# A diffusion layer's scan, projections and feed-forward: projections of the next group dealt over all steps, outputs turned a step later, low parts of weights on VectorE, and tanh of the feed-forward's first pair ahead of half the sums

## The chip, the cores and the metric

The kernel runs on one core of a Trainium2 chip. The metric is the device time of one execution in microseconds (us). The kernel before took 1807.36 us in the median of 3 runs (1804.32, 1807.36 and 1807.61). Engines are named as the profile names them: PE (TensorE matmul) and PEld (its weight loads), DVE (VectorE), ACT (ScalarE), POOL (GpSimd), SP (SyncE, which issues the DMAs).

## The reference, cut to what matters

One layer of a hybrid backbone for 640 tokens (128 of context, 512 latent), model width 1024, all in fp32:

```
h = rms_norm(x) * (1 + scale1) + shift1
q, k, v, conv_bg, conv_cg, conv_x, z, xbc, dt_raw, gate_logits = split(h @ w_in)
y_attn = blocked_attention(rope(rms_norm(q)), rope(rms_norm(k)), v) @ w_attn_o
y_conv = (conv_bg * conv3(conv_cg * conv_x)) @ w_conv_o
xs, bm, cm = split(silu(conv3(xbc) + b))          # 8 groups of 4 heads, state 128
dt = softplus(dt_raw + dt_bias)                   # the decays of the scan come from dt
y_f, s_f = ssd_chunked(xs, dt, ...)               # chunks of 128 tokens, forward
y_b, s_b = ssd_chunked(reversed, ...)             # and backward
y_ssd = rms_norm((y_f + y_b + d * xs) * silu(z)) @ w_ssd_o
x = x + gate1 * ((g_attn * y_attn + g_conv * y_conv + g_ssd * y_ssd) @ w_merge)
h = rms_norm(x) * (1 + scale2) + shift2
x = x + gate2 * ((silu(h @ w1_gate) * (h @ w1_up)) @ w2)
```

A chunk's part of the scan is a product of its C and B with the decay between each two tokens (y within the chunk), a state that the chunk adds, and C times the state that came in.

## The kernel before, in words

**Precision and tiles.** Every fp32 product is three matmuls, high by high, high by low and low by high part. `split` makes the parts: ACT casts the high part (L163), and the engine `low` subtracts it for the low part (L164), which is DVE unless the caller passes `low=pool`. Weights come in slabs of 4 × 128 × 256 through `wload` (raw tile `wr`, parts `wh` and `wl`). Tokens lie along the free axis, 640 in two halves of 320, so that a block of 256 outputs takes 2 × 8 × 3 × 2 = 96 matmuls of 128x320 (`fblock`, L297). `acc` is a pair of PSUM banks, `mx` one bank; `psum(n)` opens a pool with n of the first kind and 8 − 2n of the second.

**Order of the work.** The engines work in order, and the order on each is the one in which the program issues, save that `urgently` and `tc.high_priority()` pull an instruction forward. Where two pieces of work share PE, one is a generator (`yield` after each piece) and the other advances it with `next`. A tile of a pool with n buffers can be written when the reader of the n-th last one is done.

**The stages.** (1) 0 to 52 us: modulation and the normed h. (2) To 290 us: projections. Two plain gates, and between them `sum_forms` (L267), which makes the sums T1 to T4 of h's quarters: per block two subtractions on DVE (L274, L276) and two additions on POOL (L275, L277), and their parts. Then 12 conv units and 3 gate units go through `sunit`, a Strassen form with 7 products of 12 matmuls (L241) instead of 96; after most products DVE combines the banks into `uv` (L536 is the helper that records it, urgent). `decays()` is a generator that makes dt and what follows from it on DVE, advanced with `next(dec)` after each unit. (3) To 520 us: attention, with parts of the remaining gates, `spare`, as filling. (4) To 1047 us: the scan, in 8 groups. `group_scan(this)` (from L897) yields 9 times; its turns (`turn`, L890: x and B of a chunk, by PE), states (L912), carries of the state (`pv`, L917 and L919), weights (decay matrix `M`: a mask on POOL, L928, exponentials on ACT, L934, products on DVE), outputs (L948 and L954 on PE; y on DVE, L955 to L962) and `turn_back` (L970: y turned back by PE, two scaled copies on ACT). After each step the loop at the end advances `group_proj(g + 1)` once: a block of x0, x1, B, C or two z blocks of 24 matmuls of 128x256 (L283 to L285), seven pieces for nine steps. At step 5 `begin` turns two chunks of the next group. The last group has the spare gates beside it, three parts a step. (5) To 1268 us: the branches' output products and their merge, while `modulate()` computes the second modulation on DVE (L1074, rows `aw` from memory, two buffers). (6) To 1400 us: the merged projection, norm, and the feed-forward's first pair (gate and up of block 0) as plain halves (L1216) with `sum_forms` between, on POOL and DVE. Then `banks.close()` gives their four pairs of banks back and `psum(0)` makes eight single ones. (7) To the end: ten more pairs of blocks through `sunit` (`ff_gate`, `ff_up`) and the products down.

## Time and profile before

| | |
|---|---|
| median of 3 runs | 1807.36 us |
| profiled execution, its own time | 1801.9 us |
| its span | 1800.0 us (1.9 us lie beside it) |
| PE busy | 1731.0 us, 11924 instructions |
| DVE busy | 1280.1 us, 2256 instructions |
| ACT busy | 791.5 us |
| POOL busy | 424.5 us, 317 instructions |
| mean granted clock of PE | 0.989 |

A row of a wait reads: engine, tile and line that waited, behind the arrow what released it, then total us, times and longest. A row of a group reads: line, engine, operation, tile written and read, shape, number, then busy us and the mean ns of one, then the idle time of the engine before them and what ended it. A row of the timeline: start, length, engine, line, operation, tile, shape, number, and in brackets the idle time before it. A row `60/70/80` of a line gives the shortest, median and longest ns of one. The granted clock is a share of full speed.

### The profile page before, as it was taken

To read this page: it belongs to the slowest core of one execution; us is meant where nothing else is said; L and a number is where in the kernel's file an instruction comes from. 1 tells how busy PE (TensorE), PEld (TensorE's weight loads), DVE (VectorE), ACT (ScalarE), POOL (GpSimd) and SP (SyncE) were. 2 spreads that over 40 slices of the span, in tenths; PEclk is the share of its full clock that TensorE was granted. 3 is DMA by queue.
4 is the path that set the end of the run, shared out by engine and by line. 5 is a ranking of instruction groups with operands and counts; after the bars stand their busy time and mean duration, and the time that the engine had idled before them with its cause. 6 is when DMAs were issued, how large, how long until landed. Compare 5 with 4: busy or idle time off the path is not lost.

```text
span 1800.0 us, 30404 instructions
## 1 busy us (share of the span) xinstructions
PE 1731.0 (96%) x11924; PEld 1669.0 (93%) x11924; DVE 1280.1 (71%) x2256; ACT 791.5 (44%) x1592; POOL 424.5 (24%) x317
## 2 busy tenths in 40 slices
PE   7999999999999999999999999999997999999999
PEld 3899999999999898889889989999997999999999
DVE  5788786786546777777678557877778767767685
ACT  4534443465454665556565432122255423324240
POOL 0344451110134334333331000000004232322320
PEclk9999999999999999999999999999999999999999
DMA  7633333211243433433343378865551323223222
GB/s 286 206 101 114 111 99 115 86 42 54 77 124 111 115 100 109 140 105 102 109 130 115 110 262 269 267 194 159 172 166 48 94 59 94 71 82 95 71 89 76
DMA packets 112831, 221.76 MB, mean 123 GB/s; under 512 B 9584, under 2 KB 53488, under 8 KB 111664
## 3 DMA queue, kind: packets, MB, share of 16 engines
q1 hardware_dynamic: 112688, 219.82, 38.5%
q8 instruction: 94, 1.54, 0.3%
q14 instruction: 49, 0.40, 0.1%
HBM read 193.67 MB, written 26.12 MB: 122 GB/s over the span
## 4 chain that ended last, share of the span: by engine, by line
PE 71%; DVE 16%; DMA 7%; issue 3%; ACT 2%; POOL 1%; SPq 0%; DVEq 0%; ACTq 0%; POOLq 0%
PE mx L241 22%; PE acc L297 21%; PE mx L297 10%; DMA aw<-in_ada_dram 5%; PE mx L283 3%; PE mx L284 3%; PE mx L285 3%; DVE wl L164 2%; DVE jk L1074 2%; PE mx L912 2%; PE mx L954 1%; DVE y L961 1%; PE mx L403 1%; PE acc L725 1%; PE mx L948 1%
## 5 line engine op out<-in xcount | busy, mean ns | idle before, releaser
L297 PE MATMUL acc<-h,wh 128*128 128x320 f32 x1984 | 377.2, 312 | 0.7 <-ACT s L782 0.5
L163 ACT CAST wh<-wr 128x1024 fp32r<-128x1024 f32 (+2 forms) x226 | 218.1, 968 | 272.8 <-PE mx L241 83.8
L297 PEld LDWEIGHTS acc<-h,wh 128*128 128x128 f32 x1984 | 311.3, 189 | 1.4 <-ACT s L782 0.6
L164 DVE TENSOR_TENSOR wl<-wr,wh 128x1024 fp32r<-128x1024 f32 (+1 forms) x178 | 219.2, 1233 | 49.9 <-ACT wh L163 48.4
L297 PE MATMUL acc<-h,wl 128*128 128x320 f32 x992 | 230.1, 312 | 3.5 <-DVE wl L164 3.5
L241 PE MATMUL mx<-h,wh 128*128 128x320 f32 x840 | 188.9, 313 | 11.3 <-ACT s L163 11.3
L297 PEld LDWEIGHTS acc<-h,wl 128*128 128x128 f32 x992 | 167.1, 189 | 4.8 <-DVE wl L164 4.8
L164 POOL TENSOR_TENSOR wl<-wr,wh 128x1024 fp32r<-128x1024 f32 x48 | 119.2, 2489 | 189.4 <-ACT wh L163 183.9
L283 PE MATMUL mx<-wh,h 128*128 128x256 f32 x560 | 160.9, 287 | 1.7 <-ACT wh L163 1.0
L285 PE MATMUL mx<-wh,h 128*128 128x256 f32 x560 | 158.4, 283 | 0.0
L284 PE MATMUL mx<-wl,h 128*128 128x256 f32 x560 | 158.3, 283 | 0.0
L297 PE MATMUL acc<-s,wh 128*128 128x320 f32 x768 | 152.7, 310 | 4.3 <-issue 2.4
L241 PEld LDWEIGHTS mx<-h,wh 128*128 128x128 f32 x840 | 142.5, 190 | 11.8 <-ACT s L163 11.5
L241 PE MATMUL mx<-s,wh 128*128 128x320 f32 x640 | 141.6, 309 | 0.0
L163 ACT CAST wh<-ws 128x512 fp32r<-128x512 f32 (+1 forms) x105 | 79.7, 762 | 130.0 <-PE mx L241 71.6
L297 PE MATMUL mx<-s,wh 128*128 128x320 f32 x704 | 131.8, 309 | 0.0
L241 PE MATMUL mx<-h,wl 128*128 128x320 f32 x420 | 130.9, 312 | 0.0
L297 PEld LDWEIGHTS acc<-s,wh 128*128 128x128 f32 x768 | 123.0, 188 | 5.1 <-issue 2.7
L241 PE MATMUL mx<-T,wh 128*128 128x320 f32 x480 | 107.7, 313 | 6.9 <-DVE uv L536 6.9
L934 ACT ACTIVATE ex<-rw,nlc 128x128 f32<-128x128 f32 x320 | 101.7, 391 | 26.8 <-POOL rw L928 12.9
L1074 DVE CUSTOM_DVE_ANT_0 jk<-aw,cr 128x512 f32<-128x512 f32 x128 | 88.0, 687 | 33.2 <-DMA aw<-in_ada_dram 32.0
L297 PEld LDWEIGHTS mx<-s,wh 128*128 128x128 f32 x704 | 110.5, 188 | 0.0
(297 smaller groups left out, 3789.2 us busy)
## 6 DMA issues: line engine op xcount, KB each, us to landing
wr<-in_w_f_dram SPq DMA_DIRECT2D x64, 512.0 KB, 3.7
rw<-D_a SPq DMA_DIRECT2D x40, 512.0 KB, 5.0
aw<-in_ada_dram SPq DMA_DIRECT2D x64, 256.0 KB, 3.9
wr<-in_w_gt_dram SPq DMA_DIRECT2D x24, 512.0 KB, 4.3
wr<-in_w_cv_dram SPq DMA_DIRECT2D x24, 512.0 KB, 3.7
aw<-in_ada_dram SPq DMA_DIRECT2D x8, 1024.0 KB, 7.2
wr<-in_w_x_dram SPq DMA_DIRECT2D x16, 512.0 KB, 3.9
wr<-in_w_bc_dram SPq DMA_DIRECT2D x16, 512.0 KB, 3.7
```

Source lines behind the costliest of these rows:

```text
L163: act.copy(hi_t, src)
L164: low.tensor_tensor(lo_t, src, f32(hi_t), op=sub)
L241: pe.matmul(out, y, z, start=not more and i == 0 and j == 0, stop=i == KB // 2 - 1 and j == 2, skip_group_check=True)
L283: pe.matmul(out, l.hi, r.hi, start=start, stop=False)
L284: pe.matmul(out, l.hi, r.lo, start=False, stop=False)
L285: pe.matmul(out, l.lo, r.hi, start=False, stop=stop)
L297: pe.matmul(bank(ps, e), x, y[:, e * HT:(e + 1) * HT], start=first and i == 0 and j == 0, stop=last and i == k - 1 and j == 2)
L403: pe.matmul(pm[:n, :256], cf[:, i, :], w[:, i, :], start=i == 0, stop=i == KB - 1)
L725: pe.matmul(ps[:, e, :HT], l, r[:, P + e * HT:P + (e + 1) * HT], start=first, stop=last)
L912: pe.matmul(ps[:, d0 * GW:d1 * GW], xb[:, c, GW:], xw.pop(c)[:, d0:d1, :], start=True, stop=True)
L934: act.activation(ex[:, d, r, :], rw[:, d, r, :], AF.Exp, bias=nlc[:, c, j:j + 1])
L1074: dve.tensor_tensor_reduce(jk, aw, cr[:, s, :], 0.5, 0.0, op0=mult, op1=add, accum_out=mp[:, q, m, s:s + 1])
```

## The change

What it does, part by part:

- `sum_forms` does all four additions of a block on DVE, takes the blocks to do and tiles that it may use as scratch.
- `split` and `wload` lose `low`: the scan's low parts (48 on POOL before) are made on DVE.
- `decays` yields at two more places and after every second step of the polynomial instead of every third; the three gate units come one behind the conv blocks 1, 2 and 3 instead of within block 0.
- One pool of banks stays open through projections and attention.
- `group_proj` gives each block of x0, x1, B, C in two halves and each z block by itself: 13 pieces, dealt over the nine steps by `PARTS`. `begin` of the next group comes at step 6.
- `turn_back` of a chunk comes a step later, and y has 3 buffers.
- The last spare gate comes behind the loading of the first branch's operands (`load_set(0)`); six of these eight operands are read from memory in step 4 of the last group.
- `aw` has 4 buffers.
- In the feed-forward, the sums of blocks 0 and 1 come ahead of the second plain halves and those of 2 and 3 behind the two gates; each tanh and product follows its own halves. Block 1's gate is computed plainly (96 matmuls instead of 84) before the banks are given back.

```
-    def split(hi_t, lo_t, src, scale=None, low=dve):
+    def split(hi_t, lo_t, src, scale=None):
-            low.tensor_tensor(lo_t, src, f32(hi_t), op=sub)
+            dve.tensor_tensor(lo_t, src, f32(hi_t), op=sub)
...
-    def sum_forms(forms, quarter, new):
+    def sum_forms(forms, quarter, new, blocks=range(KB // 2), scratch=()):
+        scratch = list(scratch)
-        for i in range(KB // 2):
+        for i in blocks:
-            t12, t34 = v2(slot()), v2(slot())
+            t12, t34 = v2(scratch.pop(0) if scratch else slot()), v2(slot())
-            pool.tensor_tensor(t12[:, 1], t12[:, 0], b22, op=add)
+            dve.tensor_tensor(t12[:, 1], t12[:, 0], b22, op=add)
-            pool.tensor_tensor(t34[:, 1], b21, t12[:, 1], op=sub)
+            dve.tensor_tensor(t34[:, 1], b21, t12[:, 1], op=sub)
...
         dve.reciprocal(q, q)
+        yield
...
-            if j % 3 == 0:
+            if j % 2 == 0:
                 yield
...
         act.activation(tot, tot, AF.Exp)
+        yield
...
-                if todo:
-                    gate_unit(*todo.pop(0))
-                    next(dec, None)
+            if i:
+                gate_unit(*todo.pop(0))
+                next(dec, None)
...
-                w = wload(wsrc, low=pool)
+                w = wload(wsrc)
-                    fblock(ps, w, m, h, KB)
+                    yield from fparts(ps, w, m, 2)
...
-                if t % 2:
-                    yield
-            yield
+                yield
...
-                y = ys[c] = gp.tile([P, GW], F32, tag="y", name=nm("y"))
+                y = ys[c] = gp.tile([P, GW], F32, tag="y", name=nm("y"), bufs=3)
...
             outputs(0)
-            turn_back(4)
             weights(1)
             yield
             outputs(3)
-            turn_back(0)
+            turn_back(4)
             weights(2)
             yield
             outputs(1)
+            turn_back(0)
+            yield
+            outputs(2)
             turn_back(3)
             yield
-            outputs(2)
             turn_back(1)
             yield
             turn_back(2)
...
+        PARTS = (1, 1, 1, 2, 2, 2, 2, 1, 1)
-                next(other, None)
+                for _ in range(PARTS[n] if g + 1 < NG else 3):
+                    next(other, None)
                 if g + 1 == NG:
-                    for _ in range(2):
-                        next(spare, None)
-                elif n == 5:
+                    if n == 4:
+                        raw0 = [slot() for _ in range(6)]
+                        for k, t in enumerate(raw0):
+                            nc.sync.dma_start(t, D_o[k])
+                elif n == 6:
                     ahead = begin(g + 1, nb)
...
-                aw = mo.tile([P, HD2], F32, tag="aw", name=nm("aw"))
+                aw = mo.tile([P, HD2], F32, tag="aw", name=nm("aw"), bufs=4)
...
+run(gate_proj(*SPARE[-1]))
...
+    sums(0, 1)
     for n, (w, m) in enumerate(((wg, 0), (wg, 1), (wu, 0), (wu, 1))):
         plain_half(pss[n], w, m, 1)
+        ps = hv(pss[n])
+        if n < 2:
+            tanhs.append(slot())
+            ths.append(v2(slot(ph)))
+            urgently(act.activation, v2(tanhs[n]), ps, AF.Tanh, scale=0.5)
+            urgently(dve.scalar_tensor_tensor, ths[n], v2(tanhs[n]), 1.0, ps, op0=add, op1=mult)
+        else:
+            urgently(dve.scalar_tensor_tensor, ths[n - 2], ths[n - 2], 0.5, ps, op0=mult, op1=mult)
+        if n == 1:
+            sums(2, 3)
     hidden(0, ths)
+    wg, th = qload(w_f1[0, 1]), quads()
+    for m in range(2):
+        ps, t = acc(), th[:, 2 * m:2 * m + 2]
+        for e in range(2):
+            plain_half(ps, wg, m, e)
+        act.activation(t, hv(ps), AF.Tanh, scale=0.5)
+        dve.scalar_tensor_tensor(t, t, 1.0, hv(ps), op0=add, op1=mult)
     banks.close()
...
-    th = ff_gate(1)
```

The order on PE at the end of a group of the scan, before. In a row stand the line, the operation, the tile written and the tiles read, the shape, and how often it comes in a row. `M` is the decay matrix of the last chunk's outputs, `y` the tile that is turned back, and `acc` the first block of x of the group after the next:

```order
L954 MATMUL mx_10950<-xb_10183,M_10821 128x64 x4
L970 MATMUL mx_10967<-cst,y_10909 128x128 x2
L297 MATMUL acc_11014<-h_85,wl_11004 128x320
L297 MATMUL acc_11014<-h_87,wh_11003 128x320 x2
...
L297 MATMUL acc_11014<-h_93,wl_11010 128x320 x2
L970 MATMUL mx_10972<-cst,y_10959 128x128 x2
L938 MATMUL mx_10998<-C_10659,B_10556 128x128
```

The same place in the changed kernel (`wh` and `wl` of L284 to L286 are z's weights):

```order
L956 MATMUL mx_10885<-xb_10168,M_10708 128x64 x4
L972 MATMUL mx_10902<-cst,y_10678 128x128 x2
L284 MATMUL mx_10907<-wh_10750,h_85 128x256
...
L286 MATMUL mx_10907<-wh_10756,h_100 128x256
L972 MATMUL mx_10935<-cst,y_10798 128x128 x2
L284 MATMUL mx_10940<-wh_10750,h_85 128x256
...
L286 MATMUL mx_10940<-wh_10756,h_100 128x256
L972 MATMUL mx_10968<-cst,y_10894 128x128 x2
L940 MATMUL mx_10994<-C_10738,B_10634 128x128
```

Before, the last `y` (10959) is turned back behind 25 matmuls of the next block; now the last (10894) comes behind two z blocks, and the turn between them is of the chunk before.

The order on ACT at the feed-forward's first pair, before. `s` of L163 are the parts of the sums, `wh` those of Strassen weights, L536 the two tanh of the first pair (`acc`), and `mx` the first Strassen product:

```order
L163 CAST s_15078<-s_15067 128x320
L163 CAST wh_15213<-wr_15205 128x1024
L163 CAST s_15081<-s_15067 128x320
L536 ACTIVATE s_15180<-acc_14831 128x640
L536 ACTIVATE s_15183<-acc_14832 128x640
L163 CAST wh_15215<-ws_15208 128x512
L163 CAST s_15188<-s_15180 128x640
L163 CAST s_15192<-s_15183 128x640
L536 COPY s_15202<-mx_15231 128x320
```

And in the changed kernel, where L540 is the first pair's tanh and L1278 that of block 1's plain gate:

```order
L163 CAST s_15023<-s_15009 128x320
L540 ACTIVATE s_15068<-acc_14829 128x640
L163 CAST wh_15194<-wr_15192 128x1024
...
L540 ACTIVATE s_15096<-acc_14830 128x640
L163 CAST s_15038<-s_15027 128x320
...
L1278 ACTIVATE g_2416_15204<-acc_15205 128x640
L163 CAST wh_15323<-wr_15315 128x1024
L163 CAST wh_15325<-ws_15318 128x512
L1278 ACTIVATE g_2416_15204<-acc_15256 128x640
L540 COPY s_15312<-mx_15341 128x320
```

The two tanh stood behind the parts of all sums; now they stand among them, and a cast of weights stands ahead of the last tanh that reads the old banks.

More of the change, by code (lines that the diff above doesn't have):

```diff
@@ L183, in wraw, with wload @@
         return t[:, :b - a, :n]
-    def wload(src, k=KB, n=256, urgent=True, low=dve):
+    def wload(src, k=KB, n=256, urgent=True):
         out = []
@@ L192, in wload @@
                     pr.enter_context(tc.high_priority())
-                split(w.hi, w.lo, raw, low=low)
+                split(w.hi, w.lo, raw)
             out.append(w)
@@ L298, in fblock, with fparts @@
                               stop=last and i == k - 1 and j == 2)
-    def fparts(ps, w, m):
-        for a in range(0, KB, 2):
-            fblock(ps, w, m, h, a + 2, first=a == 0, last=a + 2 == KB, start=a)
-            if a + 2 < KB:
+    def fparts(ps, w, m, n=4):
+        s = KB // n
+        for a in range(0, KB, s):
+            fblock(ps, w, m, h, a + s, first=a == 0, last=a + s == KB, start=a)
+            if a + s < KB:
                 yield
@@ L544, in layer_kernel @@
     PLAIN, SPARE = GATES[:2], GATES[5:]
-    with tc.tile_pool(name="pj", bufs=2) as pj, psum(1):
+    banks = ExitStack()
+    banks.enter_context(psum(1))
+    with tc.tile_pool(name="pj", bufs=2) as pj:
         def quads():
@@ L859, in group_proj @@
                     yield
-            w = wload(w_z[g], low=pool)
+            w = wload(w_z[g])
             zs = out["z"] = gp.tile([P, NT, GW], F32, tag="zs", name=nm("zs"))
@@ L1233, in layer_kernel @@
     wg, wu = qload(w_f1[0, 0]), qload(w_f1[1, 0])
-    pss = [acc() for _ in range(4)]
+    accs = [acc() for _ in range(4)]
+    pss = accs[2:] + accs[:2]
     for n, (w, m) in enumerate(((wg, 0), (wg, 1), (wu, 0), (wu, 1))):
@@ L1240, in layer_kernel, with sums @@
             norm_half(1, rs)
-    sum_forms(forms, lambda n, i: hf[n][:, i], lambda: half_op(ph, "s"))
+    ths, tanhs = [], []
+    def sums(*blocks):
+        sum_forms(forms, lambda n, i: hf[n][:, i], lambda: half_op(ph, "s"), blocks, tanhs)
+    sums(0, 1)
     for n, (w, m) in enumerate(((wg, 0), (wg, 1), (wu, 0), (wu, 1))):
         plain_half(pss[n], w, m, 1)
-    ths = []
-    for ps in pss[:2]:
-        th = slot(ph)
-        urgently(act.activation, v2(th), hv(ps), AF.Tanh, scale=0.5)
-        urgently(dve.scalar_tensor_tensor, v2(th), v2(th), 1.0, hv(ps), op0=add, op1=mult)
-        ths.append(th)
-    for th, ps in zip(ths, pss[2:]):
-        urgently(dve.scalar_tensor_tensor, v2(th), v2(th), 0.5, hv(ps), op0=mult, op1=mult)
-    hidden(0, ths)
+        ps = hv(pss[n])
[8 more added lines that the diff above has]
+            sums(2, 3)
+    ths = [th.rearrange("p a b -> p (a b)") for th in ths]
+    hidden(0, ths)
+    wg, th = qload(w_f1[0, 1]), quads()
[5 more added lines that the diff above has]
+        dve.scalar_tensor_tensor(t, t, 1.0, hv(ps), op0=add, op1=mult)
     banks.close()
```

20 lines of the change are left out of this document (9 added, 11 removed).

## The prediction

> **What bounds the kernel now.** I read the page first, for the engine that sets the end.
>
> ```profile
> span 1800.0 us, 30404 instructions
> PE 1731.0 (96%) x11924; PEld 1669.0 (93%) x11924; DVE 1280.1 (71%) x2256; ACT 791.5 (44%) x1592; POOL 424.5 (24%) x317
> PE   7999999999999999999999999999997999999999
> PE 71%; DVE 16%; DMA 7%; issue 3%; ACT 2%; POOL 1%; SPq 0%; DVEq 0%; ACTq 0%; POOLq 0%
> ```
>
> PE works 1731.0 of 1800.0 us and is below nine tenths in two slices only, the first and the one at 1350–1395. So the kernel is bound by matmuls, and a change that leaves their number alone can win only PE's idle 69 us and what a slow clock costs. The second view is PE's waits (total us, times, longest), for where that idle time lies.
>
> ```profile
> PE mx L970 <- DVE y L962: 13.9, 8, 2.5
> PE mx L241 <- ACT s L163: 11.3, 1, 11.3
> PE mx L241 <- DVE uv L536: 6.9, 3, 3.6
> PE acc L297 <- DVE wl L164: 3.8, 5, 2.1
> PE acc L297 <- issue: 2.4, 1, 2.4
> PE acc L297 <- ACT s L163: 1.8, 1, 1.8
> ```
>
> In the order of the program: the 6.9 us lie in the conv and gate units of the projections, the 13.9 in the scan (the turn of a finished chunk's y waits for y), the 2.4 and 1.8 in the first branch products behind the scan, the longest of the five waits for `wl` in the merge, the 11.3 before the feed-forward's first Strassen product. Together 40.1 us; the remaining 29 are mostly the start, which the change doesn't touch. The third view is the table by stage (length; busy us of PE, weight loads, DVE, ACT, POOL; clock, DMA share, GB/s).
>
> ```profile
> 102.50:160.00 57.50, 50.62 (x324) 49.58 (x323) 53.76 (x75) 23.38 (x33) 20.65 (x15) 0.94 0.29 96
> 565.00:985.00 420.00, 405.39 (x2819) 377.02 (x2818) 307.95 (x551) 249.27 (x615) 143.95 (x107) 1.00 0.37 113
> 1047.00:1268.00 221.00, 212.93 (x1429) 210.53 (x1427) 173.14 (x359) 57.43 (x71) 0.78 (x1) 0.99 0.72 231
> 1381.50:1400.00 18.50, 7.22 (x38) 7.25 (x39) 17.18 (x21) 8.01 (x15) 8.50 (x7) 0.72 0.10 28
> ```
>
> In rows one and four DVE is full (53.76 of 57.5, 17.18 of 18.5) while PE waits; in the scan (row two, 7.3 groups of about 57.5 us) DVE has 112 us free, so a wait there is one of order and of late single instructions. Last, the clock right behind four of the waits (length, PE busy, clock, DMA).
>
> ```profile
> 144.30:150.00 5.70, 5.66 (x21) 0.50 0.32 92
> 806.40:809.40 3.00, 2.91 (x12) 0.51 0.74 279
> 1218.80:1222.00 3.20, 3.15 (x12) 0.52 0.78 233
> 1392.70:1396.00 3.30, 3.22 (x12) 0.50 0.01 2
> ```
>
> A wait costs more than itself: half the clock for 3.0 to 5.7 us behind it, that is 2.8, 1.5, 1.5 and 1.6 us.
>
> **A rule weighed.** The waits before these rows are 3.6, 2.5, 2.1 and 11.3 us. The Trainium skill, "TensorE: Matmul & The Clock Gate" (Part 1, and the table under "Why this matters for your kernels"), gives the point from which a gap costs clock as about 3 us of idle PE, a free-running window of 3413 ns. By that rule the second and third would be free, and the sum below would be 3.0 us smaller; here the clock did halve behind both, so the trace differs and I go by it.
>
> **The change, part by part.** The pace of PE and the chain into the feed-forward come from the chain of waits in order of time (start, length, link):
>
> ```profile
> 1388.48 1.23 DVE wl L164
> 1389.71 2.20 DVE s L536 x3
> 1392.78 38.84 PE mx L241 x252
> 1431.61 28.16 PE mx L297 x192
> ```
>
> 28.16 us for 192 matmuls of 128x320 is 0.1467 us each.
>
> *Projections.* The decays (dt's polynomial on DVE) come in ten pieces instead of seven, one after a unit as before, and the gate units, one behind each conv block from the second on. The three waits lie where a piece stands ahead of a unit's `uv`:
>
> ```profile
> 113.04 0.56 PE L241 MATMUL mx<-T,wh 128*128 128x320 f32 x2 [0.74 <-DVE uv L536]
> ```
>
> This first one stands before the new spacing can act: DVE's order is the same up to there, so it stays. The other two (6.1 us) and the 2.8 us of half clock go, less one us that I leave for new small waits (an estimate): −8.0. Against it stand two things on a full DVE: eight adds come from POOL, and conv units, which give DVE more work than gates, now follow each other while the pieces run. For it, no piece now has more than six instructions (the longest had seven, a reciprocal among them), and between two `uv` of one unit stand three to six of them. Ends 0 (the same waits at later units) and −9.7. That one pool of banks now stays open into the attention costs nothing: no wait for banks there is in the list.
>
> *Scan.* Two things hold y back: its place in PE's order, and DVE instructions that last six times their normal length.
>
> ```profile
> 798.28 2.36 POOL L164 TENSOR_TENSOR wl<-wr,wh 128x1024 fp32r<-128x1024 f32 x1 [1.06 <-ACT wh L163]
> 802.55 2.39 POOL L164 TENSOR_TENSOR wl<-wr,wh 128x1024 fp32r<-128x1024 f32 x1 [1.90 <-ACT wh L163]
> 803.11 2.10 DVE L961 TENSOR_TENSOR y<-y,yo 128x256 f32<-128x256 f32 x1
> 806.49 0.66 PE L970 MATMUL mx<-cst,y 128*128 128x128 f32 x2 [2.52 <-DVE y L962]
> L961 DVE TENSOR_TENSOR y<-y,yo x64: 406/416/2614, 600.5 to 1035.0; 128x256 f32<-128x256 f32 x64
> L961 DVE TENSOR_TENSOR y<-y,yo 128x256 f32<-128x256 f32 x54 | 39.7, 735 | 0.0
> L917 DVE TENSOR_TENSOR pv<-pv,cd 128x256 f32<-128x256 f32 x40 | 31.4, 784 | 3.0 <-DMA pv<-in_state_dram 2.5
> L164 DVE TENSOR_TENSOR wl<-wr,wh 128x1024 fp32r<-128x1024 f32 (+1 forms) x178 | 219.2, 1233 | 49.9 <-ACT wh L163 48.4
> L164 POOL TENSOR_TENSOR wl<-wr,wh 128x1024 fp32r<-128x1024 f32 x39 | 97.1, 2493 | 99.4 <-ACT wh L163 93.9 <-PE mx L948 5.5
> ```
>
> The y addition at 803.11 takes 2.10 us where the median is 0.416, and it ends 0.3 us behind POOL's low part, which began half a microsecond before it (0.416 and 2.614 are median and longest of 64; in the scan they average 0.735). 54 × (0.735 − 0.416) = 17 us, and L917 at the same normal length 40 × (0.784 − 0.416) = 15 us: 32 us of DVE's busy time there is standing still. In exchange 39 low parts at 1.233 us come to DVE: +48. DVE in the scan then needs 308 − 32 + 48 = 324 of 420 us, about as before, without the 2.4 us holds. The turn of the last chunk, behind 25 matmuls of x (3.7 us) now, stands behind two z blocks of 24:
>
> ```profile
> 778.70 0.36 PE L283 MATMUL mx<-wh,h 128*128 128x256 f32 x1
> 784.53 1.02 PE L948 MATMUL mx<-pv,C 128*128 128x512 f32 x2
> ```
>
> Two such blocks ran in these 5.83 us. What y needs after its matmuls, without holds, is four additions or products of 0.42 us and handing over, an estimate of 3 us; 5.8 covers that. The third buffer of y keeps the later turn from holding the next y. With a turn go its two copies on ACT (they feed nothing but the stores of y), and `begin` of the next group takes its two small state loads along on SP, a step nearer to their use; the low parts that leave POOL free its masks earlier. What gets thinner is the early steps, where x and B/C come in half blocks of 24 matmuls (3.5 us) ahead of the states instead of 48 (7.0):
>
> ```profile
> 760.68 2.45 DVE L917 TENSOR_TENSOR pv<-pv,cd 128x256 f32<-128x256 f32 x1
> 767.62 1.02 PE L912 MATMUL mx<-xw,xb 128*128 128x512 f32 x2
> ```
>
> This chain starts with a turn at 760.03, and DVE stands 2.0 of its us in the first row; its `xw` is ready 5.5 us after the turn, so 3.5 without the hold, just the 3.5 that are left. I take 1.9 us of waits as remaining (an estimate: a quarter of a microsecond in each of 7 or 8 groups): −12.0 and −1.5 of clock make −13.5. Ends: −2 (thin steps wait as long as the turns did, 1.6 us a group) and −17 (all waits, clock at two more places).
>
> *Behind the scan.* Six of the first branch's eight operands are loaded ahead, within the last group, on SP in front of y's stores; and the last gate's 96 matmuls stand between the scan's end and the first branch product, so that the 2.4 and 1.8 us lie under 14 us of PE work. The gate's banks now change hands once more, about 1 us of waiting for the last reader: −3.2. Ends 0 and −4.2.
>
> *Merge.* The second modulation's rows get four buffers instead of two.
>
> ```profile
> DVE jk L1074 <- DMA aw<-in_ada_dram: 32.0, 30, 2.7
> ```
>
> DVE waits 30 times for them, with the next `wl` in its queue behind, and one such wait reaches PE: 2.1 us and the clock's 1.5. I take both: −3.6. Ends 0 (the transfers, not the buffers, are late: the DMA share there is 0.72) and −5.3.
>
> *Feed-forward.* The banks of the first pair pass to the Strassen products only when tanh and its products on DVE have read them, and these stood behind all the sums. Now each tanh follows its own matmuls, half the sums come behind, and block 1's gate, computed plainly, fills PE: 96 × 0.1467 = 14.1 us of cover for sums that ran 11 us past PE's end. That gate is the one computed as 84 matmuls before: +12 × 0.1467 = +1.8. At its end the banks change hands again, and PE waits for tanh, a cast, a low part and the product on DVE:
>
> ```profile
> 1388.72 1.28 ACT L536 ACTIVATE s<-acc 128x640 f32<-128x640 f32 x2
> ```
>
> 0.64 for tanh, 0.73 for the product (2.20/3), up to 1.23 for the low part between: 1.4 to 3.3 with handing over, I take 2.4. Sum −11.3 − 1.6 + 1.8 + 2.4 = −8.7; ends −5 (3.3, half the clock behind it, and a microsecond of late sums) and −11.
>
> **Sum.** −8.0 − 13.5 − 3.2 − 3.6 − 8.7 = −37.0. The profiled run took 1801.9 us (1.9 beside its span), 0.3% under the median of 1807.36. So 1764.9 for such a run, and 1770.4 at the level of the median; I say 1770.
>
> **The rivals.**
> *A, the scan's waits move.* POOL keeps its masks, which read the same memory, and the steps with 24 matmuls are thin.
>
> ```profile
> L928 POOL TENSOR_SCALAR_AFFINE_SELECT rw<-rw 128x512 f32<-128x512 f32 x68 | 49.7, 754 | 171.9 <-DMA rw<-D_a 142.6 <-ACT zt L866 11.3 <-ACT xb L891 9.2
> ```
>
> For it: 3.5 us of need against 3.5 of cover. Against it: 0.75 us is the most that a mask can hold. The scan gains 2 instead of 13.5: 1782. Chance 0.14.
> *B, DVE becomes the bound of the scan: slower.* 48 us of low parts come to the engine. If the holds stay (masks, other causes) and DVE's 112 free us are waits that its order can't fill, the stretch needs 308 + 48 + 112 = 468 instead of 420: the sum loses its −13.5 and gets +48, so 1832. It decides from the point where DVE's need in a group passes PE's 57.5 us; with (308 + 48)/7.3 = 49 there is room for 8 us of waits. The Trainium skill, "Perfetto Trace Analysis" (Optimizing Scalar/DVE Operations), speaks for moving work off a saturated DVE, even to GpSimd, and adds that this might not help since the two share a read port; the rows above show the share (2.10 for 0.416), and DVE isn't full in the scan. Chance 0.05.
> *C, the last two stages give nothing, as if the change weren't there:* the transfers of the modulation are late whatever the buffers, and DVE, which now makes POOL's sums too, ends so late that PE waits its 11.3 us and loses its clock all the same. For it: DVE is busy 17.18 of 18.5 us there. Against it: 14.1 us of new cover. Then the merge's 3.6 and 11.3 − 2.4 + 1.6 = 10.5 of the feed-forward are lost: 1784. Chance 0.08.
>
> **How the numbers follow.** The forecast has 0.73. All its better ends together are 10 us more, 1760; the profiled run lay 5.5 us under the median, so 1755 is the low end. A, C and some microseconds of the other terms' worse ends (projections 8, behind the scan 3) reach to 1787; what lies above, B and A and C together, is under 2 in 10. Range 1755 to 1787. A measurement of this kernel can tell about 0.2% (3.6 us) from no change. Faster by more than that: the forecast, A and C but for a remainder, 0.92; within 0.2%: 0.03, where A and C meet and the projections give nothing; slower: B and what I haven't seen, 0.05.
>
> **What would show it.** Right: no wait of L241 for `uv` over 1 us but the first, the turns' 13.9 us under 3, L961's mean near 0.42, one wait of 2 to 3 us before the first Strassen product with PE busy in plain matmuls until then, and no half clock in the scan or the merge. Wrong: waits for `xw` or `xb` of 1.5 us a group (A), DVE over 90% busy in the scan (B), the jk waits still about 32 us with a wait for `wl` on PE, or a wait of over 5 us at the banks (C).

## The result, and the profile after

| | median us | runs | ratio to the kernel before (95% interval) |
|---|---|---|---|
| before | 1807.28 | 1804.32 to 1807.61 (4) | |
| changed | 1767.19 | 1766.39 to 1767.48 (4) | 0.9781 (0.9764 to 0.9798) |

The profiled execution of the changed kernel took 1767.09 us, at its median; that of before lay 5.4 us under its own, so the two traces differ by 34.8 us and not by 40.1. The page of the changed kernel (span and busy time, PE by slices, the chain that ended last):

```profile
span 1765.2 us, 30367 instructions
PE 1724.0 (98%) x11936; PEld 1666.4 (94%) x11936; DVE 1269.7 (72%) x2312; ACT 787.2 (45%) x1588; POOL 289.3 (16%) x249
PE   7999999999999999999999999999999999999999
PE 82%; DVE 4%; DMA 2%; issue 1%; ACT 1%; POOL 1%; DVEq 0%; POOLq 0%; ACTq 0%
```

PE's idle time fell from 69 to 41 us, the dip at 1350 to 1395 is gone, and DVE's share of the chain went from 16% to 4%. PE's waits (total us, times, longest):

```profile
PE mx L241 <- DVE uv L540: 7.1, 5, 2.4
PE mx L405 <- DMA aw<-in_ada_dram: 6.4, 1, 6.4
PE mx L241 <- DVE g L1279: 4.0, 1, 4.0
PE acc L346 <- DVE comb L385: 3.8, 1, 3.8
PE mx L914 <- DVE xw L897: 2.8, 5, 0.8
PE acc L298 <- ACT yF L974: 2.0, 1, 2.0
```

Gone are the turns (13.9 us), the wait before the first Strassen product (11.3, now 4.0 for `g`, the last product of the plain gate) and those for `wl` in the merge (3.8); in place of the 2.4 and 1.8 behind the scan stands one of 2.0 for `yF`. Not gone are the waits for `uv` in the projections: 6.9 before, 7.1 now. The table by stage at the places that answer to those shown before (length; busy us of PE, weight loads, DVE, ACT, POOL; clock, DMA share, GB/s):

```profile
102.50:160.00 57.50, 51.41 (x335) 50.36 (x334) 55.31 (x78) 20.20 (x29) 22.02 (x16) 0.97 0.25 85
561.00:965.00 404.00, 401.17 (x2820) 375.48 (x2819) 305.88 (x591) 248.67 (x621) 48.90 (x70) 1.00 0.38 117
1027.00:1240.00 213.00, 213.00 (x1457) 213.00 (x1456) 179.68 (x372) 58.04 (x72) 1.57 (x1) 1.00 0.72 237
1366.30:1385.00 18.70, 14.71 (x92) 14.45 (x91) 10.33 (x16) 6.30 (x10) 2.55 (x2) 0.91 0.19 57
```

The scan's 404 us hold 3 us of idle PE, the merge none; the first row is as full of DVE and as short of PE as before. The start of each stage in PE's timeline gives what each stage took in the two traces (the scan from its first turn to its last, the merge from there to the feed-forward's first plain half):

| stage, us | before | changed | difference | predicted |
|---|---|---|---|---|
| to the first projection | 52.4 | 53.6 | +1.2 | 0 |
| projections | 237.4 | 234.0 | −3.3 | −8.0 |
| attention, with its lead-in | 270.2 | 267.7 | −2.5 | 0 |
| scan | 479.4 | 464.0 | −15.4 | −13.5 |
| behind the scan, and merge | 311.1 | 303.0 | −8.1 | −3.2 − 3.6 |
| feed-forward | 445.4 | 438.8 | −6.6 | −8.7 |

The lengths in the experiments below are made in the same way from their own traces. The changed kernel itself did not run again beside them. Its times compare with theirs best by the ratio to the kernel before, which ran beside each, and for most of them the intervals of that ratio overlap with the changed kernel's. The lengths scatter too: traces that have the changed kernel's code in a stage took 233.6 to 235.1 us in the projections (eight traces), 460.6 to 464.7 in the scan (seven), 301 to 303 behind it (ten) and 437.2 to 439.6 in the feed-forward (nine). A difference counts below where it goes beyond these.

One slip stands above: a group of the scan had eight steps before the change, not nine; nine is the changed kernel's number.

### The profile page after: what moved, and what is told of

It reads as the page before. It is cut to its first block, busy times and chain, and to the rows that moved or that the text cites. A ratio compares the mean times of both kernels' runs of the same rounds, so it can differ in the third digit from the quotient of the medians.

```text
span 1765.2 us, 30367 instructions
## 1 busy us (share of the span) xinstructions
PE 1724.0 (98%) x11936; PEld 1666.4 (94%) x11936; DVE 1269.7 (72%) x2312; ACT 787.2 (45%) x1588; POOL 289.3 (16%) x249
## 4 chain that ended last, share of the span: by engine, by line
PE 82%; DVE 4%; DMA 2%; issue 1%; ACT 1%; POOL 1%; DVEq 0%; POOLq 0%; ACTq 0%
PE acc L298 32%; PE mx L241 20%; PE mx L298 9%; PE mx L285 3%; PE mx L286 3%; PE mx L284 3%; PE acc L1225 2%; PE mx L956 2%; PE mx L950 2%; DMA out_dram<-so 1%; PE acc L729 1%; PE mx L914 1%; PE acc L745 1%; DVE wl L164 1%; POOL rr L326 1%
## 5 line engine op out<-in xcount | busy, mean ns | idle before, releaser
L163 ACT CAST wh<-wr 128x1024 fp32r<-128x1024 f32 (+2 forms) x226 | 218.8, 971 | 298.9 <-PE acc L298 98.0
L164 DVE TENSOR_TENSOR wl<-wr,wh 128x1024 fp32r<-128x1024 f32 (+2 forms) x226 | 274.2, 1214 | 89.2 <-ACT wh L163 85.7
L241 PE MATMUL mx<-h,wh 128*128 128x320 f32 x816 | 183.3, 312 | 4.0 <-DVE g L1279 4.0
L284 PE MATMUL mx<-wh,h 128*128 128x256 f32 x560 | 160.2, 286 | 0.0
L286 PE MATMUL mx<-wh,h 128*128 128x256 f32 x560 | 158.5, 283 | 0.0
L241 PEld LDWEIGHTS mx<-h,wh 128*128 128x128 f32 x816 | 138.5, 190 | 4.5 <-DVE g L1279 4.2
L930 POOL TENSOR_SCALAR_AFFINE_SELECT rw<-rw 128x512 f32<-128x512 f32 x80 | 58.0, 749 | 479.0 <-DMA rw<-D_a 308.6
L163 ACT CAST wh<-ws 128x512 fp32r<-128x512 f32 (+1 forms) x102 | 77.2, 762 | 129.2 <-PE mx L241 65.4
L241 PE MATMUL mx<-s,wh 128*128 128x320 f32 x608 | 134.3, 309 | 0.0
L298 PE MATMUL mx<-s,wh 128*128 128x320 f32 x704 | 131.8, 309 | 0.0
L241 PE MATMUL mx<-h,wl 128*128 128x320 f32 x408 | 127.0, 311 | 0.0
L284 PEld LDWEIGHTS mx<-wh,h 128*128 128x128 f32 x560 | 107.2, 191 | 0.2 <-ACT raw L683 0.2
```

What stands on the lines that cost most here:

```text
L163: act.copy(hi_t, src)
L164: dve.tensor_tensor(lo_t, src, f32(hi_t), op=sub)
L241: pe.matmul(out, y, z, start=not more and i == 0 and j == 0, stop=i == KB // 2 - 1 and j == 2, skip_group_check=True)
L284: pe.matmul(out, l.hi, r.hi, start=start, stop=False)
L286: pe.matmul(out, l.lo, r.hi, start=False, stop=stop)
L298: pe.matmul(bank(ps, e), x, y[:, e * HT:(e + 1) * HT], start=first and i == 0 and j == 0, stop=last and i == k - 1 and j == 2)
```

## The experiments

"Holds" below is the theory that POOL's instructions stop DVE's, and "order" that the place of the work on PE brought the gain.

**The scan: which of its parts.** Four kernels ran on one chip, the kernel before taking 1803.43 us there. First the kernel before with nothing but its low parts moved to DVE:

```
-                w = wload(wsrc, low=pool)
+                w = wload(wsrc)
...
-            w = wload(w_z[g], low=pool)
+            w = wload(w_z[g])
```

> The kernel before with only the 48 low parts moved from POOL to DVE. Theory 1 (holds): y's additions average under 0.5 us instead of 0.735, the turns' waits fall from 13.9 us to under 5, and the time is 9 to 15 us below the kernel before. Theory 2 (order): the waits stay over 9 us, and the time is within 4 us of the kernel before. Theory 3 (DVE becomes the bound, rival B): slower than before.

1782.86 us, ratio 0.9884 (0.9865 to 0.9902): 20.6 us under the kernel before, more than theory 1 gave it. The scan took 460.1 us: 19.3 less than before, and 3.9 less than in the changed kernel. The additions of y in this kernel (shortest, median, longest ns of one), and its stage (columns as above):

```profile
L961 DVE TENSOR_TENSOR y<-y,yo x64: 410/419/868, 600.5 to 1015.1; 128x256 f32<-128x256 f32 x64
565.00:985.00 420.00, 419.99 (x2944) 393.05 (x2944) 321.95 (x609) 259.53 (x639) 54.22 (x70) 1.00 0.38 120
```

The longest is 0.868 us where it was 2.614, no turn waits, and PE is busy 419.99 of 420 us with the old order of steps. So moving the low parts off POOL ends all of the scan's loss, and DVE carries the 48 parts at 322 busy us of 420, where the prediction said 324. The edit also frees POOL for its masks; that it was the holds that made the turns wait shows in the trace of before. There, eight of the additions and products of y (L961 six times, L962 twice) last 2.10 to 2.61 us instead of 0.42, and no other lasts over 1.2. Each begins 0.06 to 0.57 us behind a low part of POOL's and ends 0.3 us behind it, and one of them stands in DVE's queue ahead of each of the turns' eight waits (0.8 to 2.5 us). Then the reverse, the changed kernel with the parts on POOL (`low=pool` back in the same two calls):

> The changed kernel with the scan's 48 low parts back on POOL, all else kept. Theory 1 (holds: a two-input instruction of DVE stands still while POOL's two-input instruction runs, and this is what made y and xw late): y's additions average 0.65 us or more again instead of 0.43, the waits of PE for xw at the states, which have 24 matmuls of cover, grow from 2.8 us to 8 to 14, and the time is 6 to 14 us above the changed kernel. Theory 2 (order: the later turn and the finer deal brought the scan's gain, the holds are covered): waits for xw stay under 5 us and the time is within 3 us of the changed kernel.

1807.41 us, ratio 1.0025 (1.0013 to 1.0038): a quarter of a per cent slower than the kernel before, all the rest of the change included. The loss is about three times the upper end of theory 1, and its place is another: y's additions average 0.53 us, not 0.65. PE's waits of this kernel, and DVE's and POOL's timelines ahead of the first of them:

```profile
PE mx L284 <- DVE zs L871: 20.1, 7, 3.5
...
PE mx L914 <- DVE xw L897: 5.8, 7, 1.4
```

```profile
599.48 1.08 POOL L930 TENSOR_SCALAR_AFFINE_SELECT rw<-rw 128x512 f32<-128x512 f32 x1
603.04 2.37 POOL L164 TENSOR_TENSOR wl<-wr,wh 128x1024 fp32r<-128x1024 f32 x1 [2.47 <-ACT wh L163]
```

```profile
604.76 1.46 DVE L535 SCALAR_TENSOR_TENSOR C<-s,cw,C 128x511 f32<-128x511 f32 x2 [2.31 <-ACT C L857]
606.14 1.00 DVE L536 SCALAR_TENSOR_TENSOR C<-s,cw,C 128x511 f32<-128x511 f32 x2
607.06 0.41 DVE L871 SCALAR_TENSOR_TENSOR zs<-zt,mx 128x256 f32<-128x256 f32 x1
```

`zs`, which gives z's bank back, stands in DVE's queue behind the shifts of C, and with one block of z a step, PE needs that bank at once. DVE had waited 2.31 us for ACT's C, which came late, and then the first pair of shifts, begun while POOL's part ran, took 1.46 us where the second took 1.00. The late C goes back to a hold as well (POOL, DVE and ACT):

```profile
595.75 2.59 POOL L164 TENSOR_TENSOR wl<-wr,wh 128x1024 fp32r<-128x1024 f32 x1 [2.56 <-PE mx L940]
596.94 2.09 DVE L861 SCALAR_TENSOR_TENSOR B<-s,B 128x640 f32<-128x640 f32 x1 [0.27 <-ACT s L860]
599.28 0.79 DVE L938 TENSOR_TENSOR M<-ex 128x512 f32<-128x512 f32 x1
600.15 1.87 ACT L936 ACTIVATE ex<-rw,nlc 128x128 f32<-128x128 f32 x6 [2.73 <-POOL rw L930]
```

ACT makes C behind these exponentials. The trace names POOL's mask as what they waited for, but the first mask had ended at 599.53. They begin 0.08 us behind the end of DVE's `M` (600.07), which frees one of the two tiles that they write, and so they do behind all 25 of their waits of over 1 us in this scan. `M` stands behind B's product (L861), which lasts 2.09 us beside POOL's part, and 0.82 in the mean of seven in the changed kernel. So two holds, of 1.27 and 0.46 us, lie in the chain of this wait of 2.84 us, and two like them in those of five more of the seven waits; what the rest of each is made of isn't settled. With the clock that was lost too (mean 0.984) the scan took 501.8 us. Next, the turns at their old places in the changed kernel:

```
             outputs(0)
+            turn_back(4)
...
             outputs(3)
-            turn_back(4)
+            turn_back(0)
...
             outputs(1)
-            turn_back(0)
+            turn_back(3)
             yield
             outputs(2)
-            turn_back(3)
+            turn_back(1)
             yield
-            turn_back(1)
-            yield
             turn_back(2)
+            yield
```

> The changed kernel with each turn of y back at its old step (right behind the next chunk's outputs, the last one behind one z block), all else kept. Theory 1 (holds): without holds y is there in time also at the old place; waits of the turns for y under 3 us in all, time 0 to 3 us above the changed kernel. Theory 2 (order): the turns wait 8 to 14 us again, and the time is 8 to 15 us above.

1767.75 us, ratio 0.9806 (0.9785 to 0.9826), with 2.8 us of waits for y, the longest 0.7: theory 1, though at its edge, since the scan took 467.5 us, about 3 more than the longest of the changed kernel's. And the old dealing, seven pieces, one a step (`fblock` whole, z two blocks a piece, `PARTS` all 1):

> The changed kernel with the projections of the next group in seven whole pieces, one a step, for nine steps, all else kept. Both theories: the states have 48 matmuls ahead again, so the waits for xw go (2.8 us to under 1); but the last two steps of a group have no matmuls beside them, so the last two turns wait for y, by 1.5 to 3 us a group: 7 to 15 us above the changed kernel. If the deal is worth nothing, within 2 us of it.

1768.89 us, ratio 0.9805 (0.9785 to 0.9825). The bare last steps did not cost what was expected: no turn waits for y, `xw` neither; the outputs wait 0.6 us a group for `xb`, and the scan took 466.0 us. Last, on another chip, dealing, turns, y's buffers and the step of `begin` all as before, in the changed kernel:

```
-        PARTS = (1, 1, 1, 2, 2, 2, 2, 1, 1)
+        PARTS = (1, 1, 1, 1, 1, 1, 1, 1)
...
-                elif n == 6:
+                elif n == 5:
```

> The changed kernel with the scan's dealing, the turns' places, y's buffers and the step of begin as before, and the low parts on DVE as in the change; all else as changed. Theory 1 (the holds were all of the scan's loss; the finer deal only makes the steps thin): the scan has no wait of PE over 0.3 us, a group takes 57.5 us instead of 57.6 to 58.6, and the time is 2 to 5 us under the changed kernel's 1767.2. Theory 2 (the later turn and the finer deal bring something of their own): the turns wait for y again by 0.5 us or more a group, and the time is 3 us or more above it.

1762.07 us, ratio 0.9754 (0.9723 to 0.9785); the scan 460.0 us, five of the seven distances between the groups' last turns at 57.6 us, and no wait. Theory 1: the finer deal and the later turns cost 4.0 us against the changed kernel's profiled run, and 0.6 to 4.7 against the seven traces of its order, about 3 in the mean. Putting back one of them alone doesn't win this (467.5 and 466.0 us in the two kernels before it); why it takes all four edits wasn't tried.

**The projections.** The decays and gate units as before, in the changed kernel (the two new `yield` out, `j % 3`, gate units within block 0):

> The changed kernel with the decays' pieces (seven) and the gate units' places as before; all else as changed. The prediction's step (finer pieces end the waits for uv): the projections lengthen by 4 to 8 us. Rival (the same holds, now by POOL's sums of the Strassen weights, stretch the decays' instructions wherever they stand, and which unit they meet differs from run to run): projections within 1.5 us of the changed kernel's 234.0 us, waits for uv of 5 to 8 us in all, and a time within 3 us.

1765.73 us, ratio 0.9773 (0.9735 to 0.9812). The projections took 235.5 us, and the waits for `uv` were 6.3 us, as the rival said: the finer pieces and the gate units' places bring nothing that the traces show. Then four pieces more:

```
+        yield
         n = 8
...
-            if j % 2 == 0:
-                yield
+            yield
```

> The changed kernel with the decays' polynomial in pieces of two instructions instead of four (four more pieces, all dealt by the same calls); all else as changed. If the length of a piece sets the waits for uv: they fall from 7.1 us to under 4. If holds by POOL's sums of the Strassen weights set them, of whatever DVE instruction stands ahead of uv: they stay at 5 to 8 us, and the projections at 234 us within 1.5.

1765.02 us, ratio 0.9785 (0.9769 to 0.9801); waits 6.7 us, projections 235.1 us. So the length of a piece isn't what sets the waits. The changed kernel's own timelines, POOL's and DVE's, ahead of its wait of 2.37 us at 126.22, tell why:

```profile
119.88 2.08 POOL L221 TENSOR_TENSOR ws<-ws,wr 128x512 f32<-128x512 f32 x1 [3.26 <-DVE wl L164]
122.04 1.30 POOL L222 TENSOR_TENSOR ws<-ws,wr 128x512 f32<-128x512 f32 x1
```

```profile
120.73 1.42 DVE L486 TENSOR_SCALAR s<-s 128x320 f32<-128x320 f32 x1
122.18 1.51 DVE L485 TENSOR_TENSOR s<-s,s 128x320 f32<-128x320 f32 x1
123.72 0.33 DVE L486 TENSOR_SCALAR s<-s 128x320 f32<-128x320 f32 x1
```

Two instructions of the decays end 0.2 and 0.35 us behind two sums of Strassen weights on POOL, and last 1.42 and 1.51 us; the next one, with POOL at rest, takes 0.33. These 2.1 us too much are most of the wait. So the sums of the weights were moved to DVE in the projections:

```
-    def sload(src, sp):
+    def sload(src, sp, eng=pool):
...
-            pool.tensor_tensor(s31[:, 1], r0[:, 1], r1[:, 1], op=add)
+            eng.tensor_tensor(s31[:, 1], r0[:, 1], r1[:, 1], op=add)
...
-            return sunit(src, forms, v2(slot(pj, "uv")), pj)(g), g
+            return sunit(src, forms, v2(slot(pj, "uv")), pj, dve)(g), g
```

> The changed kernel with the four additions of each Strassen unit's weights on DVE instead of POOL in the projections (POOL does nothing else there), all else as changed. If holds make the waits for uv: no DVE instruction of the decays lasts over 0.6 us there, and the waits for uv fall from 7.1 us to under 3, unless DVE, full by then with about 2.7 us more a unit, becomes the bound of the projections: then PE waits every unit, and the projections take 240 us or more instead of 234. If it is the decays' place ahead of uv, without holds: the waits stay at 5 to 8 us.

1755.33 us, ratio 0.9724 (0.9690 to 0.9758), the lowest time of this study, though its interval overlaps that of the last kernel below. No wait for `uv` is left. The stage in this kernel, and its two groups of decay instructions from 102.5 to 200 us (count, busy us, mean ns), behind them the same two of the changed kernel:

```profile
102.50:160.00 57.50, 57.50 (x395) 57.24 (x394) 55.93 (x96) 23.52 (x35) 0.00 (x0) 1.00 0.28 94
L485 DVE TENSOR_TENSOR s<-s,s 128x320 f32<-128x320 f32 x7 | 3.4, 486 | 0.1
L486 DVE TENSOR_SCALAR s<-s 128x320 f32<-128x320 f32 x7 | 2.2, 319 | 0.0
```

```profile
L485 DVE TENSOR_TENSOR s<-s,s 128x320 f32<-128x320 f32 x7 | 6.5, 926 | 0.1
L486 DVE TENSOR_SCALAR s<-s 128x320 f32<-128x320 f32 x7 | 5.3, 759 | 0.1
```

The mean of one falls from 0.926 to 0.486 and from 0.759 to 0.319 us. DVE is busy 55.93 us of 57.5 with 18 instructions more than in the changed kernel's row (55.31), and PE works all the time: a DVE that is "full" with holds has room for the work that made them. The projections took 225.5 us, 8.6 less than in the changed kernel and 8 less than in the shortest of its eight traces.

**The sums of the operands.** Two additions a block back on POOL, in the projections and the feed-forward (`pool.tensor_tensor` in the two places of `sum_forms`):

> The changed kernel with two additions a block of the sums back on POOL, in the projections and in the feed-forward; all else as changed. If POOL's additions hold DVE there as its low parts did in the scan: the stretch from the last plain half of the feed-forward's first pair to the first Strassen product grows by 1 to 5 us (the sums come later than block 1's plain gate covers), the projections by 0 to 2. If the plain gate's 14.1 us cover them anyway: within 1 us in both.

1770.19 us, ratio 0.9816 (0.9802 to 0.9831). The projections took 237.2 us (+3.1), with a wait for `uv` of 1.47 us at the first Strassen unit; the wait before the feed-forward's first Strassen product was 5.4 us instead of 4.0, and the stretch up to it 1.4 us longer. So POOL's additions cost something here too, above what was expected for the projections and at its low end for the feed-forward. How much of it is holds isn't separated: two low parts beside them last 1.17 us instead of 0.48 (at 1345.23 and 1346.32), but the additions themselves take 1.0 to 1.3 us on POOL and 0.48 on DVE, and ACT waits for them.

**The merge.** `aw` with two buffers in the changed kernel:

```
-                aw = mo.tile([P, HD2], F32, tag="aw", name=nm("aw"), bufs=4)
+                aw = mo.tile([P, HD2], F32, tag="aw", name=nm("aw"))
```

> The changed kernel with two buffers for the rows of the second modulation instead of four; all else as changed. If the buffers took the wait for wl out of the merge: that wait (about 2 us) and the half clock behind it are back, 2 to 5 us above the changed kernel, and DVE waits 25 us or more for the rows. If the earlier loads behind the scan did it, or the transfers bound it anyway: within 1 us.

1771.96 us, ratio 0.9808 (0.9778 to 0.9839). From the scan's end to the feed-forward it took 309.9 us instead of 303.0. The waits of DVE for the rows and of PE for `wl`, in this kernel:

```profile
DVE jk L1081 <- DMA aw<-in_ada_dram: 35.5, 27, 3.2
```

```profile
PE acc L298 <- DVE wl L164: 4.2, 6, 1.6
```

In the changed kernel DVE waits 0.6 us for the rows and PE never for `wl`. The buffers are worth 6.9 of that stretch's 8.1 us; 4.2 of the 6.9 are the six waits for `wl`, and no half clock came behind them. (The whole run is only 4.8 us above the changed kernel's, as its scan, of the same code, took 460.6 us.) The transfers' bound was not it: the DMA share is 0.72 in both the rows of before and after.

**The feed-forward's wait.** In the changed kernel, ACT's, DVE's and PE's timelines at the plain gate's end (its last matmul starts at 1366.30):

```profile
1366.20 1.03 ACT L163 CAST wh<-wr 128x1024 fp32r<-128x1024 f32 x1
1367.14 0.61 ACT L163 CAST wh<-ws 128x512 fp32r<-128x512 f32 x1
1367.66 0.70 ACT L1278 ACTIVATE g<-acc 128x640 f32<-128x640 f32 x1
```

```profile
1367.99 1.21 DVE L164 TENSOR_TENSOR wl<-wr,wh 128x1024 fp32r<-128x1024 f32 x1
1369.13 0.68 DVE L164 TENSOR_TENSOR wl<-ws,wh 128x512 fp32r<-128x512 f32 x1
1369.73 0.81 DVE L1279 SCALAR_TENSOR_TENSOR g<-g,acc 128x640 f32<-128x640 f32 x1
```

```profile
1370.59 0.90 PE L241 MATMUL mx<-h,wh 128*128 128x320 f32 x2 [3.99 <-DVE g L1279]
```

The last tanh stands behind two casts, the last product behind two low parts, and the banks change hands when that product ends at 1370.54. To test this, the first Strassen unit was given four banks of the old pool, and the change of pools was put behind it:

```
-        a, b, c, d = (mx()[:, :HT] for _ in range(4))
+        a, b, c, d = four or (mx()[:, :HT] for _ in range(4))
...
-    banks.close()
-    ctx.enter_context(psum(0))
...
+    four = [bank(ps, e) for ps in (acc(), acc()) for e in range(2)]
     for i in range(1, 11):
-        ff_up(i, th)
+        ff_up(i, th, four if i == 1 else None)
+        if i == 1:
+            banks.close()
+            ctx.enter_context(psum(0))
```

> The changed kernel with the first Strassen unit of the feed-forward in four banks of the old pool (free since the first pair), and the change of pools behind that unit. If the 4.0 us wait at the first Strassen product is the change of pools that waits for the last tanh and product, behind two casts and two low parts: that wait goes to under 0.5 us, one of 1 to 2.5 us comes a unit later, and the feed-forward is 2 to 4 us shorter. If the operands' sums or weights are late too: the wait stays over 2 us at the same place, and the time is the same.

1763.96 us, ratio 0.9763 (0.9731 to 0.9794). The wait is gone; three of 0.6 to 0.7 us come within that unit and behind it, and the feed-forward is 2.4 us shorter than the changed kernel's, 0.8 shorter than the shortest of its nine traces.

**Three edits together.** The scan as before with low parts on DVE, the four banks, and half of the last gate ahead of the change of pools behind the scan:

```
             run(other)
             this = ahead
+        last = gate_proj(*SPARE[-1])
+        for _ in range(4):
+            next(last)
...
-run(gate_proj(*SPARE[-1]))
+run(last)
```

> The changed kernel with three edits: the scan's dealing and turns as before with low parts on DVE (5.1 us under the changed kernel by itself), the first Strassen unit in four banks of the old pool (3.2 us by itself), and the first half of the last gate's matmuls ahead of the change of pools behind the scan. If they add: 1757 to 1760 us; the wait for yF behind the scan falls from 2.0 us to under 1.5 with no half clock behind it. If the last edit only moves the wait: 1759 to 1761.

1757.81 us, ratio 0.9747 (0.9733 to 0.9762): they add. The wait for `yF` is gone, and one of 0.80 us for the gate's tanh stands in its place. The same with the weights' sums on DVE should be faster still by the sizes above, but wasn't run.

## Why the prediction was right, point by point

The time (1770 said, 1767.19 measured) and the sign came out, in part by luck. Projections and feed-forward gave 6.8 us less than said, and scan, attention and the stretch behind the scan 5.7 us more; and one right term has a wrong reason in it. The 1770 also holds 5.5 us for the place of before's profiled run under its median: without them the forecast was 1764.9, and the changed kernel's profiled run, which lay at its median, took 1767.09.

1. *Projections, −8.0; measured −3.3.* The step that failed is "the other two go": the waits for `uv` are the same (6.9 and 7.1 us), with old pieces, new pieces and still finer ones. I had the holds in front of me in the scan and did not ask whether POOL's other two-input work does the same in the projections. It does, and taking it off POOL ends the waits and gives 8.6 us. The 3.3 themselves are hardly shown: the kernel with only the scan's low parts moved, whose projections are those of before, took 234.2 us, within the 233.6 to 235.1 of the changed ones. The operands' sums on POOL cost 3.1, in the one trace of that. My counterargument, "DVE is full", was wrong too: much of its busy time was standing still.
2. *Attention, 0; measured −2.5.* It took 267.4 to 269.7 us in twelve traces with the changed code and 270.2 and 271.0 in two with the old. In the changed kernel the one wait of 1.0 us at its first weights is gone, and those for `pr` (1.3 to 0.8) and `rms` (0.7 to 0.2) are 0.5 us shorter each; why isn't traced.
3. *Scan, −13.5; measured −15.4.* The holds were right and undersized: the parts on DVE alone give −19.3, all that the scan had to give. The later turn, which I counted as needed cover, gives nothing of its own, and the finer deal costs what I feared from thin steps (2.8 us of waits for `xw`, where I took 1.9): the new order as a whole +3.9, or 0.6 to 4.7 by the other traces. An order without holds needs no more cover than the old one had.
4. *Behind the scan −3.2, merge −3.6; measured −8.1 together.* The sum is right within 1.3 us, the shares are not. The buffers give 6.9: there were several waits for `wl`, where I priced one and its clock. The earlier loads leave about 1.2, no more than traces of one code differ by here (1.0 to 1.8), since the change of pools waits 2.04 us for `yF` (I took 1) and loses clock, below.
5. *Feed-forward, −8.7; measured −6.6.* The mechanism was right. The term that was too small is the wait at the banks, 2.4 said and 4.0 measured: I had put one cast and up to one low part ahead of it, and there were two of each. The half clock behind it, which I had at the far end only, came too (0.67 over 4.5 us, 1.5 us). The two are 3.1 us against a miss of 2.1; the difference isn't traced.

Of the rivals, A was true for 2.8 us of waits and not for the scan's gain; its 0.75 us, "the most that a mask can hold", was the mean of the masks, and the longest took 1.34 in the trace of before. B stayed away: DVE is busy 306 of 404 us in the scan. With the parts back on POOL the new order does become slower than before, but not because DVE is full (330 of 502 us busy): late instructions stand in its queue ahead of those that PE needs. C was wrong in both halves: DVE waits 0.6 us for the rows, and PE 4.0 for the banks instead of 11.3 for the sums.

## What to carry to other kernels

An instruction whose length varies six times for one shape is the first thing to look for: compare the median and the longest of a group, lay the long ones beside the other engines' timelines, and then look for the same partner in every stage, not only in the one where the wait is largest. Busy time with holds in it is no measure of an engine's load: here DVE took over work twice, and its busy time hardly rose (308 to 322 us in 420 of the scan, 55.3 to 55.9 in 57.5 of the projections). The changed kernel still has such a partner in the feed-forward: at 1349.98, 1351.46, 1357.95 and 1359.46, DVE's parts and sums of 0.48 us last 1.56 to 1.58 beside POOL's sums of the Strassen weights, and taking those off POOL there wasn't run. And a reordering that gives a late result more cover should be tried again once the lateness is cured, since it can then cost more than it gives.

## What the runs showed of the hardware

A `TENSOR_SCALAR` of DVE with a single tile to read (L486, 128x320) is held like one that reads two: 1.42 us beside POOL's sum, 0.33 without. The `uv` combinations, which read one operand from a bank of PSUM, are not held: 0.47 to 0.48 us in the mean in the same stretch. Of these and the `g` that are made like them, 20 ran beside an instruction of POOL's in the changed kernel's projections, and none took over 0.50 us; L485, with two tiles to read, took 0.48 in the mean of four without POOL and 1.52 in that of three beside it. The Trainium skill, "SBUF — State Buffer" (Who interferes with whom), gives two cases in which a DVE instruction contends with GpSimd: two inputs from SBUF, and modes that take both ports, which a `tensor_scalar` can enter; in the second, whoever issues first blocks the other for the whole instruction. The trace agrees that both kinds are held; which mode the `TENSOR_SCALAR` ran in it doesn't show.

The clock halves behind short waits in some places and not in others (length, PE busy, clock, DMA share, in the changed kernel):

```profile
126.00:131.00 5.00, 4.78 (x22) 0.66 0.29 105
142.20:147.20 5.00, 4.94 (x34) 1.00 0.30 105
1021.90:1025.50 3.60, 3.55 (x14) 0.53 1.05 323
1370.50:1375.00 4.50, 4.41 (x21) 0.67 0.32 107
```

The waits ahead of these rows were 2.37, 1.92, 2.04 and 3.99 us. Other traces show that the length alone doesn't decide. In the kernel with the weights' sums on DVE the same wait behind the scan was again 2.04 us, and the clock stayed at 1.00; in the one with only the low parts moved, a wait of 1.86 us in the merge was enough:

```profile
1014.62 0.85 PE L298 MATMUL acc<-h,wh 128*128 128x320 f32 x4 [2.04 <-ACT yF L974]
1014.60:1018.20 3.60, 3.58 (x24) 1.00 1.03 331
```

```profile
1242.09 0.56 PE L297 MATMUL acc<-h,wl 128*128 128x320 f32 x2 [1.86 <-DVE wl L164]
1242.10:1246.10 4.00, 4.00 (x18) 0.62 0.69 242
```

In the kernel before, the clock was 1.00 over the 4.9 us behind the wait of 2.52 us at 128.14, and in the one with the turns at their old places over the 4.5 us behind 3.74 us at the change of pools in the feed-forward. So a wait of under 2 us can be enough, below the about 3 us that the page of the Trainium skill cited in the prediction gives, and one of 3.7 us can cost no clock; what decides between them isn't shown.
